# A transformer block's FFN on one core: SiLU as one ACT activation in half 1 and in the block products, and five plain weights split ahead instead of three

## The chip, the core and the metric

The kernel runs on one core of a Trainium2 chip. The core has five engines that the profile shows: PE (TensorE: matmuls, and PEld for their weight loads), DVE (VectorE), ACT (ScalarE), POOL (GpSimd) and SP, whose queue starts the DMA transfers here. Each engine works through its own queue in order; an instruction that waits holds up everything behind it in that queue. The metric is device time in microseconds (us), the median of several runs; lower is better.

## The reference, cut to what matters

The program computes one layer: sparse attention and an RWKV mixer, a gated merge, an output projection, and then the FFN, which alone the change touches:

```python
def _conv_ffn(h, w_up, conv_w, w_down):
    u = h @ w_up                       # 1024 x 1024 by 1024 x 5632
    u = conv(u, conv_w)                # causal, 3 taps, each channel by itself
    a, b = jnp.split(u, 2, axis=-1)    # 2816 channels each
    return (jax.nn.silu(a) * b) @ w_down
...
x = x + _conv_ffn(_rms_norm(x, norm_ffn[l]), ffn_up[l], ffn_conv[l], ffn_down[l])
```

SiLU is x times sigmoid(x), which is also 0.5 x (1 + tanh(x / 2)).

## The kernel before, in words

All products are made of float16 parts: an operand is split into hi (rounded) and lo (the rest), and each product is three matmuls, hi by hi, hi by lo and lo by hi. A weight tile of 128 x 1024 is loaded by SP into a raw buffer (`wraw`, two buffers in each of two pools), ACT writes its hi (`whi`, line 1602 in `split8`), and DVE its lo (`wlo`, line 1603). For the first two plain weights POOL makes the lo.

The FFN's 22 pairs of channel tiles (a tile of "a" channels with the matching tile of "b" channels) are worked in this way. The sequence of 1024 positions has two halves of 512.

- For pairs 0 to 5 (NE = 6) the halves are done apart, as plain products. Half 0 is filler work in earlier stages (`ffn0`, line 892 is its tanh). **Half 1** is the loop over `i in range(NE)`: per pair two plain weights (one of "a", one of "b"), each 24 matmuls; `taps` reads the result from PSUM into a tile u (ACT line 1529, two DVE taps line 1532, an edge line 1534); `silu` makes th = silu(ua) * ub with a tanh on ACT (1540) and two passes on DVE (1541, 1542), and SP stores th. u tiles have two buffers a kind. The weights come from `wslot`, which hands out pairs of hi and lo buffers in turn; PFD of them are split before the loop, and each step asks for one more. In the same loop DVE and ACT make the T tiles (`tprep`, lines 1557, 1558 and 1563): sums and differences of activations, split into hi and lo.
- For pairs 6 to 21 both halves go through **block products**: a scheme with seven half-size products instead of eight, each a group of 12 matmuls (`prod`, line 1669). The profile's PE rows carry the operands' names, so the groups of a product can be told apart. In PE's order they are: (1) weight "a" by h2h (`whi` by `h2h`); (2) `s12h` by T1; (3) the group `whi` by T4, which belongs to the "b" weight of the product before and is held back until here; (4) `s12h` by T2; (5) "a" by the second h2h; (6) `s34h` by T3; (7) `s34h` by `h2hi`.
- Between the groups ACT copies PSUM banks: line 1718 (bank b0 from a0, which group 4 adds to), 1721 (p5), 1725 (the **seed copy**, bank a1 from b0, after group 4 and before group 6 overwrites b0), 1733 (u3). DVE adds u3 and p5 in (1734, 1736), after which "a" of the product is complete and its taps start: U on ACT (1691), two taps on DVE (1693). `last`, a generator that is kept until the next product (`pend`), does the same for "b" and then makes TH = silu(U0) * U1 over all 1024 positions: tanh on ACT (1705), two passes on DVE (1706, 1707), two stores on SP (1709).
- The weights of the next products are prepared meanwhile by `prep_up`: it loads raw "a" and "b", POOL forms the sums s12 (1625, 1626) and s34 (1629, 1630), and `split8` splits "a", s12, s34 and the second half of "b" (a 128 x 512 `whi` and `wlo`). The buffers `whi`/`wlo` alternate between "a" and "b"; a raw buffer is free for a later load when its last reader has run.

Then the down projection follows, with its own weights and products (lines 1801 and 1872).

The order of the instructions in each engine's queue is made by a planner at build time: it takes the program's order as priority and places each instruction when it is ready by the planner's own model of durations. `tc.issue_after(x)` forces the instructions in its block to stand behind x in the queue of x's engine; it is an order, not a wait across engines. Inside the loop over the products the calls stand like this (shortened):

```python
prod(b0, w["12"], 4, TB[2], False)               # group 4
seed = A.activation(a1, b0, AF.Copy).ins         # 1725
if pend:
    next(pend)                                   # TH of the product before
wn = next(g_)                                    # raw loads, split of the next "a"
prod(a0, w["a"], 4, b21, False)                  # group 5
```

Of the kernel before, what the change touches and what calls it, by code (L numbers as in the profile page):

```python
# [11 lines left out]
AF = mybir.ActivationFunctionType  # L12
ALU = mybir.AluOpType
# [52 lines left out]
LV = 20  # L66
NEW = 4
TSTEPS = [(0, 0), (0, 1), (1, 1), (2, 2), (2, 3), (3, 3)]
PFD = 3
DSEQ = "nnsnsnsn"  # L70
GD = 6
GT = 7
# [96 lines left out]
def build(tc, D, dbg=None, upto=99):  # L169
    nc = tc.nc  # L170
    V, A, G, T = nc.vector, nc.scalar, nc.gpsimd, nc.tensor
# [5 lines left out]
    with ExitStack() as ctx:  # L177
        def pool(name, bufs=1, space=None, stack=ctx, **kw):
            if space is not None:
                kw["space"] = space  # L180
            return stack.enter_context(tc.tile_pool(name=name, bufs=bufs, reuse_waits="tile", **kw))
# [1343 lines left out]
        fp = pool("ffn", 1, stack=fst)  # L1525
# [11 lines left out]
        def silu(i, h, ua, ub):  # L1537
            th = fp.tile([128, 512], F32, name="th", tag="TH", bufs=2)
            with tc.issue_after(lasts[0]):
                t_ = A.activation(th, ua, AF.Tanh, scale=0.5)  # L1540
            V.scalar_tensor_tensor(th, th, 1.0, ua, op0=ALU.add, op1=ALU.mult)
            V.scalar_tensor_tensor(th, th, 0.5, ub, op0=ALU.mult, op1=ALU.mult)
            nc.sync.dma_start(th_d[h][i], th)
            return t_.ins

        lasts = [None]

# [35 lines left out]
        def wraw(src, scale="A", behind=None):  # L1583
            rn_[0] += 1
            x_ = rn_[0] // 2 % 2
            raw = (wp, fp)[x_].tile([128, 8, 128], F32, name="wraw", bufs=2)
            lastw[0] = load(raw, src).ins
            if scale == "A":
                with tc.issue_after(behind) if behind is not None else ExitStack():
                    A.activation(raw, raw, AF.Copy, scale=WS)  # L1590
            elif scale == "G":
                G.tensor_scalar(raw, raw, WS, 0.0, op0=ALU.mult, op1=ALU.add)
            return raw

        def split8(raw, ph, pl, th, tl, ks=slice(0, 8), e=None, **kw):
            hi = ph.tile([128, 8, 128], F16, name=th, **kw)
            lo = pl.tile([128, 8, 128], F16, name=tl, **kw)
            if e is G:
                lasts[0] = A.activation(hi[:, ks], raw[:, ks], AF.Copy).ins
                G.tensor_sub(lo[:, ks], raw[:, ks], hi[:, ks])  # L1600
            else:
                lasts[0] = A.activation(hi[:, ks], raw[:, ks], AF.Copy, scale=WS).ins  # L1602
                V.scalar_tensor_tensor(lo[:, ks], raw[:, ks], WS, hi[:, ks], op0=ALU.mult, op1=ALU.subtract)  # L1603
            return hi, lo

        wn_ = [0]

        def wslot(src):
            n = wn_[0] % 4
            wn_[0] += 1  # L1610
            e = V if WV[0] <= wn_[0] < WV[1] and wn_[0] % WV[2] == 0 else G
            raw = wraw(src, "G" if e is G else None)
            if n % 2 == 0:
                return split8(raw, wp, wp, "whi", "wlo", bufs=2, e=e)
            return split8(raw, fp, fp, ("s12h", "s34h")[n // 2], ("s12l", "s34l")[n // 2], e=e, bufs=2)

        lo4, hi4 = slice(0, 4), slice(4, 8)

        def prep_up(i):
            ra, rb = ((fp, wp)[i % 2].tile([128, 8, 128], F32, name="wraw", bufs=2) for _ in range(2))  # L1620
            load(ra, D["f_up"][i])
            lastw[0] = load(rb, D["f_up"][22 + i]).ins
            w = {"a": split8(ra, wp, wp, "whi", "wlo", bufs=2)}
            s12, s34 = (fp.tile([128, 8, 128], F32, name=n_) for n_ in ("s12", "s34"))
            G.tensor_add(s12[:, lo4], rb[:, lo4], rb[:, hi4])  # L1625
            G.tensor_sub(s12[:, hi4], s12[:, lo4], ra[:, lo4])  # L1626
            yield w
            w["12"] = split8(s12, fp, fp, "s12h", "s12l", bufs=2)
            G.tensor_sub(s34[:, lo4], ra[:, lo4], rb[:, lo4])  # L1629
            G.tensor_sub(s34[:, hi4], ra[:, hi4], s12[:, hi4])  # L1630
            yield
            w["34"] = split8(s34, fp, fp, "s34h", "s34l", bufs=2)
            yield
            w["b"] = split8(rb, wp, wp, "whi", "wlo", hi4, bufs=2)
            yield

        wq = [wslot(D["f_up"][22 * (n % 2) + n // 2]) for n in range(PFD)]
        for i in range(NE):
            us = []
            if i == NE - 1:  # L1640
                g_ = prep_up(NE)
                w = next(g_)
                next(g_)
            pjs = [ps("APMB"[(2 * i + o) % 4]) for o in range(2)]
            if i == 0 and LOL[3]:
                run(mm3s(list(zip(pjs, wq[:2])), h2hi[1], h2lo[1], 8, 1))
            for o in range(2):
                n = 2 * i + o + PFD
                if n < 2 * NE:
                    wq.append(wslot(D["f_up"][22 * (n % 2) + n // 2]))  # L1650
                hi, lo = wq.pop(0)
                u = utile(o, 1)
                pj = pjs[o]
                if i or not LOL[3]:
                    run(mm3(pj, hi, lo, h2hi[1], h2lo[1], 8))
                lasts[0] = taps(u, o, i, 1, pj)
                us.append(u)
            if i:
                silu(i - 1, 1, *prev)
            prev = us  # L1660
            with tc.issue_after(lasts[0]):
                for k in TSTEPS[i]:
                    next(tg[k])
        silu(NE - 1, 1, *prev)

        def prod(bank, w, o_, xs_, start):
            n = 0
            for k, wi, xi in [(k, 0, x_) for k in range(4) for x_ in (0, 1)] + [(k, 1, 0) for k in range(4)]:
                T.matmul(bank, w[wi][:, o_ + k], xs_[k][xi], start=start and n == 0, stop=n == 11,  # L1669
                         skip_group_check=True)  # L1670
                n += 1
# [13 lines left out]
        def wide(name):  # L1685
            return fp.tile([128, 1024], F32, name=name, tag=name, bufs=2)

        def taps2(o, i, c):
            ci = 22 * o + i
            u = wide(f"U{o}")  # L1690
            A.activation(u, c, AF.Copy, scale=P("conv", 88 + ci))  # L1691
            for d in (1, 2):
                V.scalar_tensor_tensor(u[:, d:1024], c[:, 0:1024 - d], P("conv", 44 * (2 - d) + ci), u[:, d:1024],  # L1693
                                       op0=ALU.mult, op1=ALU.add)
            return u
# [3 lines left out]
        def last(i, w, ua, cc):  # L1699
            b0 = cc[:, 0:512]  # L1700
            prod(b0, w["b"], 4, TB[4], False)
            ub = taps2(1, i, cc)
            yield
            th = wide("TH")
            lt_[0] = A.activation(th, ua, AF.Tanh, scale=0.5).ins
            V.scalar_tensor_tensor(th, th, 1.0, ua, op0=ALU.add, op1=ALU.mult)
            V.scalar_tensor_tensor(th, th, 0.5, ub, op0=ALU.mult, op1=ALU.mult)
            for h in range(2):
                nc.sync.dma_start(th_d[h][i], th[:, H[h]])
            yield  # L1710

        pend, lt_ = None, [None]
        for i in range(NE, 22):
            g_ = prep_up(i + 1) if i < 21 else iter([None] * 4)
            ca, cb_ = (pall[:, b_:b_ + 1024] for b_ in (1024 * (i % 2), 2048 + 1024 * (i % 2)))
            a0, a1, b0, b1 = ca[:, 0:512], ca[:, 512:1024], cb_[:, 0:512], cb_[:, 512:1024]
            prod(a0, w["a"], 0, b11, True)
            A.activation(b0, a0, AF.Copy)
            prod(b1, w["12"], 0, TB[1], True)
            p5 = fp.tile([128, 512], F32, name="p5")  # L1720
            A.activation(p5, b1, AF.Copy)
            if pend:
                next(pend)
            prod(b0, w["12"], 4, TB[2], False)
            seed = A.activation(a1, b0, AF.Copy).ins
            if pend:
                next(pend)
            wn = next(g_)
            prod(a0, w["a"], 4, b21, False)
            next(g_)  # L1730
            prod(b0, w["34"], 0, TB[3], False)
            u3 = fp.tile([128, 512], F32, name="u3")
            A.activation(u3, b0, AF.Copy)
            V.tensor_add(b1, b1, u3)
            prod(a1, w["34"], 4, b22, False)
            V.tensor_add(a1, a1, p5)
            pend = last(i, w, taps2(0, i, ca), cb_)
            next(g_)
            next(g_)
            w = wn  # L1740
        run(pend)
        t_ = lt_[0]
# [245 lines left out]
```

## Time and profile before

| | |
|---|---|
| median of 3 runs (lowest to highest) | 1710.64 us (1709.13 to 1712.36) |
| the profiled execution, its whole time | 1718.26 us |
| its span, first to last instruction | 1716.3 us |
| mean granted clock of PE, whole span | 0.986 |
| PE / DVE / ACT / POOL busy | 1646.6 / 1196.7 / 917.1 / 431.6 us |
| half 1's products | from about 1125 to 1187 us |
| block products | from 1188.6 to about 1494 us |

Times in rows are counted from the span's start. In a timeline a row gives start, length, engine, line, operation, output and inputs; square brackets give the idle time just before and what ended it. "issue" there means that the engine waited for nothing that the profile shows. A row of a group gives busy time and mean ns of one after the bar. Matmuls are pipelined: the length of one (0.38 us) runs over the start of the next.

### The profile page before, as it was taken

How to read it: one execution, taken by the hardware profiler on the slowest of the kernel's cores; microseconds unless marked ns; L12 is line 12 of the kernel's file. 1: busy time of each engine (PE TensorE's matmuls, PEld its weight loads, DVE VectorE, ACT ScalarE, POOL GpSimd, SP SyncE). 2: the span in 40 equal slices, each digit the busy share in tenths (PEclk: the TensorE clock that was granted, in tenths of full speed). 3: DMA queues.
4: the chain of work that ended last, by engine and by line, in shares of the span. 5: the costliest groups of instructions: out<-in, count | busy, mean ns of one | idle time of the engine just before them, and what ended most of it. 6: DMA issues, size and time to landing. Idle time of an engine off the chain costs nothing.

```text
span 1716.3 us, 30297 instructions
## 1 busy us (share of the span) xinstructions
PE 1646.6 (96%) x11856; PEld 864.1 (50%) x11856; DVE 1196.7 (70%) x1978; ACT 917.1 (53%) x1625; POOL 431.6 (25%) x352
## 2 busy tenths in 40 slices
PE   8999999999999999998989999999999999999997
PEld 3446555555555545665655534444444444444443
DVE  6545577778876657954446585499867777786898
ACT  6664675757667645455446464454444544645530
POOL 2101131121112110000004200123333333456756
PEclk9999999999999999998999999999999999999999
DMA  6242343242444474435345673543222222534402
GB/s 221 91 136 90 96 145 115 78 135 60 130 141 134 129 235 156 137 118 173 124 143 184 205 280 104 175 151 129 86 86 74 81 92 87 213 113 129 135 25 99
DMA packets 124687, 224.62 MB, mean 131 GB/s; under 512 B 16384, under 2 KB 45440, under 8 KB 124416
## 3 DMA queue, kind: packets, MB, share of 16 engines
q1 hardware_dynamic: 124544, 222.69, 39.4%
q8 instruction: 93, 1.52, 0.4%
q14 instruction: 50, 0.41, 0.1%
HBM read 153.86 MB, written 63.96 MB: 127 GB/s over the span
## 4 chain that ended last, share of the span: by engine, by line
PE 40%; DVE 11%; DMA 7%; ACT 5%; issue 4%; POOL 4%; DVEq 0%; POOLq 0%; SPq 0%; ACTq 0%
PE pall L271 15%; PE pall L1801 5%; PE pall L1669 5%; PE pall L1872 4%; PE pall L291 2%; DMA wraw<-f_up 2%; DMA zs<-sg_d 2%; POOL s L1629 1%; PE pall L1220 1%; POOL s L1625 1%; DVE s12l L1603 1%; PE pall L1164 1%; POOL s L1626 1%; PE pall L1311 1%; DVE wlo L1603 1%
## 5 line engine op out<-in xcount | busy, mean ns | idle before, releaser
L271 PEld LDWEIGHTS <-whi 128*128 128x128 f16 x1840 | 177.3, 98 | 211.5 <-issue 14.7
L271 PE MATMUL pall<-hlo,whi 128*128 128x512 f16 x608 | 229.6, 379 | 2.1 <-DVE hlo L246 2.1
L271 PE MATMUL pall<-hhi,whi 128*128 128x512 f16 x608 | 229.1, 379 | 2.0 <-ACT ad L981 1.5
L261 DVE SCALAR_TENSOR_TENSOR wlo<-wraw,whi 128x1024 f16<-128x1024 f32 (+1 forms) x98 | 111.0, 1133 | 65.3 <-ACT whi L259 35.9
L271 PE MATMUL pall<-hhi,wlo 128*128 128x512 f16 x608 | 154.5, 382 | 0.0
L665 DVE TENSOR_TENSOR pl<-pf,ph 128x512 f16<-128x512 f32 (+3 forms) x208 | 117.3, 573 | 36.9 <-ACT pf L664 36.2
L259 ACT ACTIVATE whi<-wraw 128x1024 f16<-128x1024 f32 (+1 forms) x98 | 92.7, 948 | 91.7 <-PE pall L271 66.8
L271 PEld LDWEIGHTS <-wlo 128*128 128x128 f16 x920 | 88.0, 98 | 100.1 <-issue 4.6
L663 ACT ACTIVATE ph<-pall 128x512 f16<-128x512 f32 (+3 forms) x208 | 99.6, 479 | 64.6 <-PE pall L658 32.7
L600 DVE TENSOR_REDUCE mp<-pall 128x1 f32<-128x512 f32 (+2 forms) x192 | 95.8, 515 | 35.6 <-PE pall L598 26.3
L664 ACT ACTIVATE pf<-pall 128x512 f32<-128x512 f32 (+3 forms) x208 | 100.0, 481 | 0.0
L1693 DVE SCALAR_TENSOR_TENSOR U<-pall,par,U 128x1023 f32<-128x1023 f32 x64 | 82.0, 1282 | 8.1 <-ACT U L1691 6.2
L1625 POOL TENSOR_TENSOR s<-wraw 128x512 f32<-128x512 f32 x16 | 25.7, 1608 | 220.5 <-DMA wraw<-f_up 207.5
L1602 ACT ACTIVATE s12h<-s 128x1024 f16<-128x1024 f32 x16 | 16.9, 1057 | 95.9 <-POOL s L1626 94.9
L1393 POOL TENSOR_TENSOR b<-b,bonus 128x512 f32<-128x512 f32 x8 | 10.7, 1343 | 224.7 <-ACT b L1391 196.7
L668 PEld LDWEIGHTS <-ph 128*128 128x128 f16 x592 | 56.1, 97 | 16.0 <-ACT ph L663 2.8
L673 PEld LDWEIGHTS <-pl 128*128 128x128 f16 x592 | 55.9, 99 | 15.8 <-DVE pl L665 7.1
L687 POOL TENSOR_TENSOR onat<-onat,ot 128x256 f32<-128x256 f32 x32 | 27.6, 868 | 138.9 <-DVE ot L686 109.3
L1669 PEld LDWEIGHTS <-whi 128*128 128x128 f16 x384 | 37.5, 98 | 46.7 <-ACT u L1529 1.7
L671 PEld LDWEIGHTS <-ph 128*128 128x128 f16 x592 | 56.2, 98 | 6.0 <-issue 1.7
L1803 DVE SCALAR_TENSOR_TENSOR acc<-pall,acc 128x512 f32<-128x512 f32 x80 | 51.8, 678 | 8.6 <-PE pall L1801 8.5
L1603 DVE SCALAR_TENSOR_TENSOR wlo<-wraw,whi 128x1024 f16<-128x1024 f32 (+1 forms) x37 | 50.4, 1362 | 1.9 <-PE pall L1669 1.2
(596 smaller groups left out, 4469.7 us busy)
## 6 DMA issues: line engine op xcount, KB each, us to landing
wraw<-f_up SPq DMA_DIRECT2D x56, 512.0 KB, 3.4
wraw<-w_t SPq DMA_DIRECT2D x46, 512.0 KB, 3.8
wraw<-f_dn SPq DMA_DIRECT2D x22, 512.0 KB, 3.8
sg_d<-zs SPq DMA_DIRECT2D x32, 256.0 KB, 2.2
wraw<-w_out SPq DMA_DIRECT2D x16, 512.0 KB, 3.6
th_d<-TH SPq DMA_DIRECT2D x32, 256.0 KB, 2.3
z_d<-zs SPq DMA_DIRECT2D x28, 256.0 KB, 2.9
x<-xT SPq DMA_DIRECT2D x24, 256.0 KB, 5.6
```

What stands on the lines that cost most here:

```text
L259: A.activation(hi[:, :nk], raw, AF.Copy, scale=WS)
L261: V.scalar_tensor_tensor(lo[:, :nk], raw, WS, hi[:, :nk], op0=ALU.mult, op1=ALU.subtract)
L271: lastm[0] = T.matmul(ps, a[:, k], ks_(b, k), start=(n == 0), stop=(n == 3 * nk - 1)).ins
L600: V.reduce_max(mp[:, x, br, t:t + 1], pm[:, 0:(b1 - b0) * 128], axis=AX.X)
L663: A.activation(ph[0:nkey, rg], pa[0:nkey, rg], AF.Exp, scale=0.125)
L664: A.activation(pf[0:nkey, rg], pa[0:nkey, rg], AF.Exp, scale=0.125)
L665: V.tensor_sub(pl[0:nkey, rg], pf[0:nkey, rg], ph[0:nkey, rg])
L1603: V.scalar_tensor_tensor(lo[:, ks], raw[:, ks], WS, hi[:, ks], op0=ALU.mult, op1=ALU.subtract)
L1669: T.matmul(bank, w[wi][:, o_ + k], xs_[k][xi], start=start and n == 0, stop=n == 11, skip_group_check=True)
L1693: V.scalar_tensor_tensor(u[:, d:1024], c[:, 0:1024 - d], P("conv", 44 * (2 - d) + ci), u[:, d:1024], op0=ALU.mult, op1=ALU.add)
L1801: T.matmul(pj, x[:, m], y, start=(n == 0), stop=(n == 5))
L1872: T.matmul(pj, w[x][:, 4 * kp + j], hs[kp][y], start=(n == 0), stop=(n == 5))
```

## The change

Three edits. In half 1 and in the block products the tanh and the two DVE passes become one SiLU activation on ACT and one plain product on DVE. In the block products that SiLU is made to stand behind the seed copy of the product in which it runs (`lt_[1]`); before, the tanh had no such place. And PFD goes from 3 to 5, with `wslot` handing out buffers in a round of three (whi, s12, s34, two buffers each) where it was a round of four (whi, s12, whi, s34). Half 0 (`ffn0`) keeps its tanh.

```diff
-PFD = 3
+PFD = 5
...
         def silu(i, h, ua, ub):
             th = fp.tile([128, 512], F32, name="th", tag="TH", bufs=2)
             with tc.issue_after(lasts[0]):
-                t_ = A.activation(th, ua, AF.Tanh, scale=0.5)
-            V.scalar_tensor_tensor(th, th, 1.0, ua, op0=ALU.add, op1=ALU.mult)
-            V.scalar_tensor_tensor(th, th, 0.5, ub, op0=ALU.mult, op1=ALU.mult)
+                A.activation(th, ua, AF.Silu)
+            V.tensor_mul(th, th, ub)
             nc.sync.dma_start(th_d[h][i], th)
-            return t_.ins
...
         def wslot(src):
-            n = wn_[0] % 4
+            n = wn_[0] % 3
             wn_[0] += 1
             e = V if WV[0] <= wn_[0] < WV[1] and wn_[0] % WV[2] == 0 else G
             raw = wraw(src, "G" if e is G else None)
-            if n % 2 == 0:
+            if n == 0:
                 return split8(raw, wp, wp, "whi", "wlo", bufs=2, e=e)
-            return split8(raw, fp, fp, ("s12h", "s34h")[n // 2], ("s12l", "s34l")[n // 2], e=e, bufs=2)
+            return split8(raw, fp, fp, ("s12h", "s34h")[n - 1], ("s12l", "s34l")[n - 1], e=e, bufs=2)
...
             th = wide("TH")
-            lt_[0] = A.activation(th, ua, AF.Tanh, scale=0.5).ins
-            V.scalar_tensor_tensor(th, th, 1.0, ua, op0=ALU.add, op1=ALU.mult)
-            V.scalar_tensor_tensor(th, th, 0.5, ub, op0=ALU.mult, op1=ALU.mult)
+            with tc.issue_after(lt_[1]):
+                lt_[0] = A.activation(th, ua, AF.Silu).ins
+            V.tensor_mul(th, th, ub)
             for h in range(2):
                 nc.sync.dma_start(th_d[h][i], th[:, H[h]])
             yield
...
-        pend, lt_ = None, [None]
+        pend, lt_ = None, [None, None]
...
-            seed = A.activation(a1, b0, AF.Copy).ins
+            seed = lt_[1] = A.activation(a1, b0, AF.Copy).ins
```

## The prediction

> **What bounds the kernel now.** I read the page's head first, then the busy time by stretch, the waits of PE, PE's and ACT's timelines over one block product, and the chain of waits there.
>
> ```profile
> span 1716.3 us, 30297 instructions
> PE 1646.6 (96%) x11856; PEld 864.1 (50%) x11856; DVE 1196.7 (70%) x1978; ACT 917.1 (53%) x1625; POOL 431.6 (25%) x352
> ```
>
> PE bounds the whole: about 70 us of the span are without a matmul, and only what lies in the FFN can be won here. The stretches (span; then PE, PEld, DVE, ACT, POOL busy; clock; DMA share; GB/s):
>
> ```profile
> 1185.00:1205.00 20.00, 14.17 (x65) 6.01 (x64) 20.00 (x26) 10.33 (x15) 10.23 (x7) 1.00 0.45 159
> 1205.00:1285.00 80.00, 80.00 (x372) 36.29 (x371) 59.51 (x52) 35.63 (x46) 25.12 (x16) 1.00 0.26 89
> 1285.00:1470.00 185.00, 179.34 (x817) 79.74 (x816) 137.92 (x119) 86.31 (x111) 58.62 (x37) 1.00 0.25 86
> 1470.00:1700.00 230.00, 227.90 (x1050) 102.55 (x1049) 184.35 (x236) 107.75 (x164) 149.30 (x107) 1.00 0.32 109
> ```
>
> The clock is full, so lost time is waiting. PE stands at two places: at the passage from half 1 into the block products (5.8 us of 20) and in the later block products (5.7 of 185). What PE waited for between 1130 and 1520 us, longest first (line, releaser: total, times, longest):
>
> ```profile
> PE pall L1669 <- ACT pall L1725: 4.4, 10, 0.4
> PE pall L1669 <- ACT pall L1718: 1.9, 1, 1.9
> PE pall L1669 <- DVE T2l L1558: 1.9, 1, 1.9
> ```
>
> The ten waits for L1725, the seed copy, are one per block product, and they understate the loss. PE's first matmuls of a product, of its second group, and of the next product:
>
> ```profile
> 1338.79 0.38 PE L1669 MATMUL pall<-h2h,whi 128*128 128x512 f16 x1
> ...
> 1341.38 0.38 PE L1669 MATMUL pall<-T1h,s12h 128*128 128x512 f16 x1
> ...
> 1357.82 0.38 PE L1669 MATMUL pall<-h2h,whi 128*128 128x512 f16 x1
> ```
>
> A group of 12 matmuls takes 2.59 us, so seven groups need 18.13; the product takes 19.03. Each of ten products loses 0.9, together **8.9 us**. At the passage the four standstills, with the 0.16 by which a matmul's modelled end runs on (0.38 against 2.59/12 = 0.22), come to 5.8 + 4 x 0.16 = **6.5 us**. So 15.4 us is all this change can win by waiting less.
>
> Why 19.03? The chain of waits over the same time shows a ring (start, length):
>
> ```profile
> 1332.24 0.70 DVE wlo L1603
> 1332.93 0.02 issue
> 1332.95 3.16 DMA wraw<-f_up
> ...
> 1336.28 1.82 POOL s L1625
> 1338.09 2.21 POOL s L1629
> 1340.30 1.24 POOL s L1626
> ...
> 1341.56 1.07 ACT s12h L1602
> ...
> 1342.65 1.31 DVE s12l L1603
> 1343.96 0.61 DVE pall L1734
> 1344.57 0.61 DVE pall L1736
> ```
>
> wlo of the 512-wide "b" weight is the last reader of a raw buffer. Its end starts the load of a later weight, POOL sums that, ACT and DVE split the sum, and only behind that split, in DVE's order, come the additions L1734 and L1736 that finish the running product. ACT goes on:
>
> ```profile
> 1326.18 1.11 ACT L1691 ACTIVATE U<-pall,par 128x1024 f32<-128x1024 f32 x1 [1.16 <-DVE pall L1736]
> 1327.19 0.59 ACT L1718 ACTIVATE pall<-pall 128x512 f32<-128x512 f32 x1
> 1330.01 1.06 ACT L1705 ACTIVATE TH<-U 128x1024 f32<-128x1024 f32 x1 [2.23 <-issue]
> 1330.97 0.58 ACT L1721 ACTIVATE p<-pall 128x512 f32<-128x512 f32 x1
> 1331.45 0.62 ACT L1602 ACTIVATE whi<-wraw 128x512 f16<-128x512 f32 x1
> 1331.97 1.11 ACT L1691 ACTIVATE U<-pall,par 128x1024 f32<-128x1024 f32 x1
> 1332.97 0.60 ACT L1725 ACTIVATE pall<-pall 128x512 f32<-128x512 f32 x1
> ```
>
> The tanh (L1705) waits 2.23 us for DVE's two taps, and p, whi of "b", the U of "b" and the seed stand behind it on ACT. DVE puts its first tanh product ahead of wlo too. That closes the ring at 19.02 (wlo 1332.24, next 1351.26): it, and not PE, sets the pace.
>
> **The change, part by part.**
>
> (1) *The block products' SiLU behind the seed.* ACT loses nothing in count (one activation for one), but p, whi of "b", U and seed no longer wait for the taps. Count from a product's first matmul. The fourth group starts at 3 x 2.59 = 7.77; the third, which reads the old wlo of "b", ends there, so wlo cannot be written sooner. It now can be written just then, at 7.8: whi stands ahead of U on ACT and p is long free, and DVE is through its taps, which take
>
> ```profile
> 1327.33 2.60 DVE L1693 SCALAR_TENSOR_TENSOR U<-pall,par,U 128x1023 f32<-128x1023 f32 x2
> ```
>
> from 1.15 after U's start. Before, wlo began at 1351.26 - 1338.79 = 12.5, so it comes 4.7 us earlier. From wlo's start to the next U is 1345.20 - 1332.24 = 13.0 (U stands one period of 19.02 behind 1326.18), and from there to the end of L1718 1327.78 - 1326.18 = 1.6. So L1718 ends at 7.8 + 14.6 = 22.4, that is 4.2 into the next product; PE wants it at 7.77. **The ring has 3.5 us to spare, and PE paces itself at 18.13.**
>
> What is late next? The seed, after the fourth group (10.4), ends at 11.0 and PE wants it at 12.95. The SiLU runs 11.0 to 12.0, whi of the next "a" behind it to 13.1, and wlo of "a", behind DVE's TH product (12.1 to 13.3), by 16.1 (2.8 us, an estimate: the 0.70 of the half-wide wlo, doubled for the width and again for a slow neighbour); PE wants that at 18.13 + 8 x 0.22 = 19.9. The two stores of TH follow the product on SP; the load that waits for "a"'s wlo stands behind them and has a whole product to land. The SiLU itself is no operation of the trace: nearest is the tanh of the same shape (1.06), which I take; at twice that, the spare 3.8 us still cover it. Gain 8.9, if the queues come out like this; bounds 0 and 8.9.
>
> (2) *One product for two on DVE.* Per block product one pass goes. It had 1.3 us apiece:
>
> ```profile
> L1707 DVE SCALAR_TENSOR_TENSOR TH<-TH,U 128x1024 f32<-128x1024 f32 x16 | 21.1, 1320 | 0.5
> ```
>
> DVE is free for 47 of 185 us there, so beyond the ring this is worth nothing. In half 1 it counts, for there DVE is full:
>
> ```profile
> 1112.00:1208.00 96.00, 90.17 (x417) 40.48 (x416) 95.62 (x131) 50.10 (x77) 30.04 (x16) 1.00 0.42 142
> ```
>
> 95.6 of 96 us, and the standstills at the passage are waits for what DVE brings late (T1l and T2l directly, the bank copies through u tiles that its products hold). Five SiLUs lie before the last of them:
>
> ```profile
> L1542 DVE SCALAR_TENSOR_TENSOR th<-th,u 128x512 f32<-128x512 f32 x5 | 5.5, 1110 | 0.0
> L1541 DVE SCALAR_TENSOR_TENSOR th<-th,u 128x512 f32<-128x512 f32 x5 | 3.9, 779 | 0.0
> ```
>
> A plain product for the pair frees between 3.9 and 5.5, less the 0.07 that neighbours overlap: 3.5 to 5.1. I take 3.6, the low end: L1542 has the shape of L1541 and is longer by 0.33, which I put down to POOL working beside it, and that will slow another pass instead.
>
> (3) *Five weights ahead.* No instruction is added or removed. The twelve plain weights go round whi, s12, s34 with two buffers each; whi alone, every second turn, had held it to four. The later weights are split up to two products (2 x 24 x 0.216 = 10.4 us) sooner, their raw buffers come free sooner, and with them the loads, POOL sums and splits of the first block product, on which ACT stood blocked with u copies behind it. But DVE is full, so what moves forward pushes taps and T tiles back: I count it at 0, between -3 (the order hurts T2l) and +2.9 (all 6.5 gone, with (2)).
>
> (4) *The table.* One load at the first SiLU, near 1148:
>
> ```profile
> L1501 ACT ACT_TABLE_LOAD x1 | 1.3, 1283 | 0.0
> ```
>
> ACT is half idle there (50 of 96), so 0; uncovered, 1.3. The ACT rows above show tanh among copies without a load between. The Trainium skill ("ScalarE: Activation LUTs", Table sets: the hidden batching unit) tells to batch activations by set, since each switch costs a load, and that cheap functions such as copy are in every set. By the first half, read alone, the change would be a loss; by the second, one switch suffices. Its price (same page, What ACT_TABLE_LOAD costs) is 2.66 us with the drain; by that the sum would move by nothing or, uncovered, 2.7.
>
> **Sum:** 8.9 + 3.6 + 0 + 0 = 12.5 us. From 1470 PE is busy 227.9 of 230 us, so the gain reaches the end whole. The profiled execution took 1718.26 (span 1716.3), 7.6 above the median of the runs, 1710.64, so it would come to 1705.8, and the median to **1698**.
>
> **Rivals.**
>
> *A: only the loop gains.* The passage stays DVE's, its 3.6 eaten by the new order or worse, down to -3: gain 5.9 to 8.9, 1702 to 1705. For: DVE is full. Against: work really goes away. Taps of "b" ahead of its wlo land here too: wlo starts at 8.9 + 2.6 = 11.5, the ring needs 18.3, a loss of about 0.2 a product. So does a table that lacks copy: two loads of 1.3 per SiLU put the split of "a" at 18.7, still before 19.9, and hurt half 1 alone; if they take half of the 6 x 2.6 us from where ACT is late, the passage's 3.6 and 4 more are gone, 1706.
>
> *B: the ring stays.* Another in-order neighbour takes the tanh's place, and the product still takes 18.9; only the passage gains: 1707. For: DVE's and ACT's order is the planner's and is planned anew. Against: every member is ready earlier.
>
> *C: slower.* On DVE the TH product lands ahead of wlo of "b" (or its stores ahead of that weight's load on SP). Then wlo hangs on the seed: from the fourth group, 2.59 + 0.6 + 1.1 + 1.2 + 14.6, with some 0.2 of hand-over, is 20.3 against 18.13. That bites from about the third product on: 13 x 2.1 = 27 lost for 8.9 before, less 3.6: +15, 1725. It decides once wlo starts over 3.5 us after the third group. For: the tanh product stands ahead of wlo today. Against: it stands there because it was ready first; now wlo is ready at 7.8, the product at 12.0.
>
> **How the numbers follow.** Forecast 0.70, A 0.10, B 0.09, C 0.11. What can be told from no change is 0.2%, 3.4 us. Forecast and A are faster (0.80), B the same (0.09; it lies at the edge), C slower (0.11). The forecast's own range is 1694 (all 15.4 and a little) to 1702; with A and B it ends at 1710. C stays out.
>
> **What would show it.** Right: PE's starts of successive products 18.1 apart to the end; no wait for L1725; wlo of "b" within 1 us of the third group's end; no standstill over 1 us at the passage; DVE some 0.6 us less per half-1 SiLU; one more table load. Wrong: a product still near 19, or DVE holding wlo for the TH product.

## The result, and the profile after

| | before | after |
|---|---|---|
| first comparison, median (lowest to highest) | 1711.14 us (1709.13 to 1712.36), 4 runs | 1701.01 us (1699.11 to 1703.55), 4 runs |
| ratio, 95% interval | | 0.9943 (0.9926 to 0.996) |
| second comparison, median (lowest to highest) | 1711.87 us (1708.77 to 1716.88), 11 runs | 1698.15 us (1694.59 to 1700.95), 6 runs |
| ratio, 95% interval | | 0.9916 (0.990 to 0.9933) |
| profiled execution of the first: whole time, span | 1718.26, 1716.3 us | 1703.55, 1701.8 us |

The change makes the kernel faster, by 10.1 us in the first comparison and 13.7 in the second. The forecast was 1698, 12.5 less than before.

The head of the page of the changed kernel:

```profile
span 1701.8 us, 30292 instructions
...
PE 1640.8 (96%) x11856; PEld 863.7 (51%) x11856; DVE 1174.4 (69%) x1956; ACT 923.3 (54%) x1626; POOL 435.6 (26%) x352
```

DVE works 22.3 us less in 22 instructions fewer (one pass for two, 6 + 16 times), ACT has one instruction more, a table load. The same stretches as before, each moved to where the work now lies (span; then PE, PEld, DVE, ACT, POOL busy; clock; DMA share; GB/s):

```profile
1183.00:1203.00 20.00, 17.66 (x82) 7.81 (x81) 18.35 (x26) 8.45 (x13) 7.05 (x5) 1.00 0.51 172
1203.00:1283.00 80.00, 80.00 (x372) 36.28 (x371) 57.94 (x49) 39.94 (x49) 27.93 (x16) 1.00 0.24 86
1283.00:1468.00 185.00, 185.00 (x859) 83.87 (x857) 133.47 (x111) 93.86 (x114) 64.45 (x37) 1.00 0.27 95
1468.00:1690.00 222.00, 219.74 (x1011) 98.63 (x1009) 176.92 (x231) 100.34 (x154) 149.85 (x109) 1.00 0.31 109
```

In the stretch of 185 us PE now has no idle time at all, where 5.7 us were lost. At the passage it is idle for 2.3 us of 20, where it was 5.8. What PE waited for between 1130 and 1520 us:

```profile
PE pall L1667 <- DVE T1l L1556: 1.9, 1, 1.9
PE pall L1667 <- ACT pall L1716: 0.5, 1, 0.5
```

The ten waits for the seed copy are gone. PE's first matmul of the second group in three products one behind another:

```profile
1297.36 0.38 PE L1667 MATMUL pall<-T1h,s12h 128*128 128x512 f16 x1
...
1315.49 0.38 PE L1667 MATMUL pall<-T1h,s12h 128*128 128x512 f16 x1
...
1333.62 0.38 PE L1667 MATMUL pall<-T1h,s12h 128*128 128x512 f16 x1
```

18.13 and 18.13: seven groups of 2.59 without a gap, and so to the last product.

For the comparisons below I add up PE's standstills from the start of half 1 to the end of the block products: the time from one matmul's start to the next, less the usual 0.22. Before, that is 6.49 us at the passage and 8.81 in the loop, 15.30 together; after, it is 2.65 and 0. **12.65 us went.** The span fell by 14.5, because half 1 also began 1.35 us sooner (its first matmul at 1122.04 for 1123.39), which is well within what this start moves between two executions of one kernel (last section). From the second group of the last product to the end it is 241.7 us before and 241.2 after, so nothing is given back later.

### The profile page after: what moved, and what is told of

Same layout as the page of the kernel before. It is cut to its first block, busy times and chain, and to the rows that moved or that the text cites. A ratio compares the mean times of both kernels' runs of the same rounds, so it can differ in the third digit from the quotient of the medians.

```text
span 1701.8 us, 30292 instructions
## 1 busy us (share of the span) xinstructions
PE 1640.8 (96%) x11856; PEld 863.7 (51%) x11856; DVE 1174.4 (69%) x1956; ACT 923.3 (54%) x1626; POOL 435.6 (26%) x352
## 5 line engine op out<-in xcount | busy, mean ns | idle before, releaser
L271 PEld LDWEIGHTS <-whi 128*128 128x128 f16 x1808 | 173.6, 98 | 205.6 <-issue 11.4
L1667 PEld LDWEIGHTS <-whi 128*128 128x128 f16 x384 | 37.6, 98 | 45.3 <-issue 0.2
```

Source lines behind the costliest of these rows:

```text
L271: lastm[0] = T.matmul(ps, a[:, k], ks_(b, k), start=(n == 0), stop=(n == 3 * nk - 1)).ins
```

## The experiments

"Passage" and "loop" are the two sums of standstills just defined; a standstill repeats closely (2.65 and 2.66 at the passage in two profiled executions of the changed kernel), while the whole time of one execution moves by several us for another reason (last section). So where a kernel was run only once, its verdict rests on the standstills. They are sums of waits alone; what the table leaves out in e1, e5 and e9 stands behind it.

| kernel | half 1 | block products | plain weights ahead | passage | loop | products apart |
|---|---|---|---|---|---|---|
| before | tanh, 2 passes | tanh, no place | 3 | 6.49 | 8.81 | 19.02 later |
| after | SiLU | SiLU behind seed | 5 | 2.65 | 0 | 18.13 |
| e1 | tanh, 2 passes | tanh behind seed | 3 | 6.54 | 0 | 18.13 |
| e2 | SiLU | SiLU, no place | 5 | 2.65 | 8.74 | 19.02 later |
| e8 | SiLU | SiLU ahead of p | 5 | 2.68 | 8.58 | 19.02 later |
| e10 | tanh, 2 passes | tanh (behind p), sums' splits later | 3 | 3.56 | 0 | 18.13 |
| e3 | SiLU | SiLU behind seed, wlo of "b" behind TH | 5 | 2.67 | 0.45 | 18.13 |
| e9 | SiLU | tanh, no place | 3 | 3.97 | 8.45 | 19.02 later |
| e5 | tanh, 2 passes | SiLU behind seed | 5 | 4.06 | 0 | 18.13 |
| e4 | SiLU | SiLU behind seed | 3 | 2.19 | 0 | 18.13 |
| e7 | SiLU | SiLU behind seed, T tiles first | 5 | 1.49 | 0 | 18.13 |
| e11 | SiLU | SiLU behind seed, T tiles first | 3 | 2.04 | 0 | 18.13 |

In the single executions of e1, e5 and e9 the granted clock also stood at one half for 3.4 us, right behind a standstill at the passage (from 1206.9, 1193.0 and 1197.7 us). In e1 (behind the busy times: clock, DMA share, GB/s):

```profile
1207.00:1210.00 3.00, 3.00 (x9) 1.07 (x8) 0.29 (x1) 0.00 (x0) 0.00 (x0) 0.50 0.00 0
```

Matmuls began 0.43 us apart there instead of 0.22, which cost another 1.6 us in each of the three. With it the passage lost 8.2 us in e1, 5.7 in e5 and 5.6 in e9. Before the change and in e10, with standstills of 2.1 us at the same place, the clock stayed at 1.00. Each of the three was run once, so whether these 1.6 us belong to their edits is open, and the comparisons at the passage below are given with and without them.

**The order alone.** The old kernel, with its tanh and two passes, and only the place behind the seed added:

```diff
-            lt_[0] = A.activation(th, ua, AF.Tanh, scale=0.5).ins
+            with tc.issue_after(lt_[1]):
+                lt_[0] = A.activation(th, ua, AF.Tanh, scale=0.5).ins
...
-            seed = A.activation(a1, b0, AF.Copy).ins
+            seed = lt_[1] = A.activation(a1, b0, AF.Copy).ins
```

> The kernel before with one edit: in the block products the tanh is put behind the seed copy; tanh and both DVE passes stay, half 1 and the weights too. Theory (the place of the activation closes or opens the ring): products 18.1 us apart, no waits for the seed copy, about 8.9 us less; the passage keeps its 6.5 us. Rival (it is DVE's saved pass that frees the ring): products stay at 19.0.

The stretch of 185 us in the loop, and what PE waited for from half 1 to the end of the products:

```profile
1285.00:1470.00 185.00, 185.00 (x859) 83.86 (x858) 156.11 (x123) 93.74 (x115) 73.05 (x37) 1.00 0.27 94
```

```profile
PE pall L1669 <- ACT pall L1726: 2.8, 1, 2.8
PE pall L1669 <- ACT pall L1719: 1.9, 1, 1.9
PE pall L1669 <- ACT u L1529: 1.2, 1, 1.2
```

The whole loss of the loop is gone with both DVE passes still there (DVE is busy for 156 of 185 us, more than before). The three waits left are single ones, all at the passage, and come to what the passage lost before. One execution took 1708.83 us, beside 1710.9 for the kernel before; that is less than the 8.8 us of standstill that went. Of the difference 1.6 us are the half clock at the passage; more cannot be read from one execution each.

**The order taken away.** The changed kernel without the place for its SiLU, and, as a second run, with the SiLU put expressly where the tanh of before stood, ahead of p and whi of "b":

```diff
-            with tc.issue_after(lt_[1]):
-                lt_[0] = A.activation(th, ua, AF.Silu).ins
+            lt_[0] = A.activation(th, ua, AF.Silu).ins
```

> The changed kernel without the order behind the seed copy: the planner places the block products' SiLU by itself; in the order it made, the SiLU stands behind whi of 'b' and ahead of U of 'b' and of the seed. Theory: wlo of 'b' no longer hangs on the SiLU, so the ring (about 16.7 us by its members) stays under PE's 18.13 and products are 18.1 apart, as in the changed kernel. Rival (the stated order itself is what gains): back to 18.9 to 19.0, about 8 us more than the changed kernel.

```diff
+            th = wide("TH")
+            lt_[0] = A.activation(th, ua, AF.Silu).ins
+            yield
             prod(b0, w["b"], 4, TB[4], False)
             ub = taps2(1, i, cc)
             yield
-            th = wide("TH")
-            with tc.issue_after(lt_[1]):
-                lt_[0] = A.activation(th, ua, AF.Silu).ins
...
-            A.activation(p5, b1, AF.Copy)
+            if pend:
+                next(pend)
+            with tc.issue_after(lt_[0]) if pend else ExitStack():
+                A.activation(p5, b1, AF.Copy)
```

> The changed kernel with the SiLU at the tanh's old place on ACT: ahead of p, whi of 'b', U of 'b' and seed. One DVE pass as in the changed kernel. Theory: the ring is U to taps 3.8, SiLU 1.1, p 0.5, whi 0.6, wlo to the next U 13.0, together 18.9, over PE's 18.13, so products drift to 18.9 apart once the slack of 3.5 us is used up (some five products), and 6 to 8 us are lost against the changed kernel. Rival (the saved DVE pass is what matters): 18.1 apart, no loss.

Both go back to 19.02, and lose 8.74 and 8.58 us in the loop. For the first of them I had misjudged the order: behind whi of "b" is where the SiLU stood in the first product, the only one I had looked at, while in the later ones the planner put it where the tanh had been. ACT in a later product of that kernel (left to the planner):

```profile
1336.93 0.59 ACT L1715 ACTIVATE pall<-pall 128x512 f32<-128x512 f32 x1
1339.75 1.06 ACT L1703 ACTIVATE TH<-U 128x1024 f32<-128x1024 f32 x1 [2.23 <-issue]
1340.71 0.58 ACT L1718 ACTIVATE p<-pall 128x512 f32<-128x512 f32 x1
1341.19 0.62 ACT L1600 ACTIVATE whi<-wraw 128x512 f16<-128x512 f32 x1
```

Again 2.23 us of waiting for the taps, with p and whi behind it. And the chain of waits of the second kernel (SiLU expressly ahead of p), over one turn of the ring:

```profile
1340.14 0.53 ACT whi L1600
...
1340.69 0.70 DVE wlo L1601
...
1341.41 3.13 DMA wraw<-f_up
...
1344.71 1.98 POOL s L1623
1346.68 2.21 POOL s L1627
1348.89 1.23 POOL s L1624
...
1359.71 0.70 DVE wlo L1601
```

From wlo to wlo 19.02, as in the kernel before, although DVE has no tanh product ahead of wlo any more. So the pass that the change saves in the loop buys nothing there while the ring is closed: the ring closes over ACT, and the order is the whole gain of the loop. One execution each took 1708.78 and 1706.94 us, beside 1710.9 before.

**The ring shortened at another place.** The old kernel, with its tanh still ahead of whi of "b", its U and the seed; the splits of s12 and s34 are ordered behind the additions of the running product, so that these additions no longer wait for the loaded weight:

```diff
-            next(g_)
+            with tc.issue_after(fin[0]) if fin else ExitStack(), tc.issue_after(fin[1]) if fin else ExitStack():
+                next(g_)
...
-            A.activation(u3, b0, AF.Copy)
+            uc = A.activation(u3, b0, AF.Copy).ins
...
-            V.tensor_add(a1, a1, p5)
+            fin = uc, V.tensor_add(a1, a1, p5).ins
```

> The kernel before with another link of the ring cut: tanh and two passes stay at the old place, but the split of s12 is put behind the additions (u3 copy on ACT, the second addition on DVE) of the product before. In the order made, both sums' splits stand between the additions and U's taps. Theory: additions and U (2.3 us) leave the ring, the split of s34 (1.2) enters: 19.0 - 2.3 + 1.2 = 17.9, just under PE's 18.13, so products are 18.1 to 18.3 apart and 7 to 9 us are gained in the loop; the passage keeps about 6.5. Rival (the tanh's place delays PE through the seed copy alone, with no ring): products stay at 19.0.

```profile
1285.00:1470.00 185.00, 185.00 (x858) 83.83 (x857) 134.91 (x120) 97.59 (x119) 64.58 (x39) 1.00 0.27 97
```

In this stretch PE has no gap, and the products stand 18.13 apart to the end. DVE in one product:

```profile
1328.62 0.70 DVE L1737 TENSOR_TENSOR pall<-pall,p 128x512 f32<-128x512 f32 x1 [1.26 <-PE pall L1669]
1329.23 1.22 DVE L1603 SCALAR_TENSOR_TENSOR s12l<-s,s12h 128x1024 f16<-128x1024 f32 x1
```

The addition now waits for PE, and the split comes behind it. The ring is not open, for on ACT the next U (1330.17) still stands behind the splits s12h and s34h (1327.86 and 1329.21); but it closes in less than PE's 18.13, since whi of "b" waits for PE in it, by 0.19 us (1335.53). Shortened at another member, the same ring frees the loop as the change does. That is the strongest support for the ring as the cause: no SiLU is in this kernel, and its tanh still holds up whi of "b". The planner did put the tanh behind p. By itself that would take the 0.5 us of p (1330.97 to 1331.45 before) out of 19.02 and leave about 18.5, an estimate, still above 18.13. The kernel has a gain at the passage too, 3.56 for 6.49, which I had not looked for. One execution took 1701.41 us, beside 1710.9.

**wlo of "b" held behind the TH product**, the order of rival C:

```diff
-            V.tensor_mul(th, th, ub)
+            lt_[2] = V.tensor_mul(th, th, ub).ins
...
+            if late:
+                with tc.issue_after(lt_[2]):
+                    next(late)
...
-            next(g_)
+            late = g_
```

> The changed kernel with wlo of 'b' forced behind the TH product on DVE, the order of rival C. The planner answers by placing the split of s12 behind the additions and U's taps, so that additions and U no longer wait for POOL. Theory (only the ring counts, and this order opens it at the split): products 18.13 apart, no loss. Rival C as priced (a late wlo costs whatever the rest of the order): 20.2 apart, some 25 us more than the changed kernel.

DVE over one product of it:

```profile
1300.96 1.23 DVE L1705 TENSOR_TENSOR TH<-TH,U 128x1024 f32<-128x1024 f32 x1 [0.41 <-ACT TH L1704]
1302.10 1.82 DVE L1601 SCALAR_TENSOR_TENSOR wlo<-wraw,whi 128x512 f16<-128x512 f32 x2
1305.19 0.70 DVE L1735 TENSOR_TENSOR pall<-pall,u 128x512 f32<-128x512 f32 x1 [1.27 <-ACT u L1734]
...
1309.04 2.60 DVE L1691 SCALAR_TENSOR_TENSOR U<-pall,par,U 128x1023 f32<-128x1023 f32 x2 [1.18 <-ACT U L1689]
1312.30 1.31 DVE L1601 SCALAR_TENSOR_TENSOR s12l<-s,s12h 128x1024 f16<-128x1024 f32 x1 [0.66 <-ACT s12h L1600]
```

wlo does stand behind the TH product, and the products still come 18.13 apart. But the planner, given the later weight, also put s12l behind the additions and the taps: the order of the experiment before. The 0.45 us lost in its loop is one gap, before a matmul of the down projection. So this run does not test the price of C (1725 us), which supposed the rest of the order unchanged; it shows that one late member costs nothing once the additions are out of the ring. A late wlo with the additions still behind s12l was not tried. One execution took 1698.18 us, beside 1713.46.

**The passage, edit by edit.** The SiLU of half 1 alone on the old kernel; then the changed kernel with the old half 1 (and five weights ahead); then the changed kernel with three weights ahead:

```diff
-                t_ = A.activation(th, ua, AF.Tanh, scale=0.5)
-            V.scalar_tensor_tensor(th, th, 1.0, ua, op0=ALU.add, op1=ALU.mult)
-            V.scalar_tensor_tensor(th, th, 0.5, ub, op0=ALU.mult, op1=ALU.mult)
+                A.activation(th, ua, AF.Silu)
+            V.tensor_mul(th, th, ub)
```

(The second run takes these lines back from the changed kernel.) And the third, against the changed kernel:

```diff
-PFD = 5
+PFD = 3
...
-            n = wn_[0] % 3
+            n = wn_[0] % 4
...
```

> The kernel before with the SiLU and one pass in half 1 alone; three weights ahead, block products as before. Theory: the ring is untouched, late products 19.02 apart; the passage stands 2.5 to 3.5 us instead of 6.5, and from half 1's first matmul to the last block product 3 to 4 us are saved, as the ring starts sooner too. Rival (the ring takes the passage's gain back, since its first U comes no sooner): under 1 us saved over that stretch.

> The changed kernel with half 1's tanh and two DVE passes back; five weights ahead and the block products' SiLU stay. Products 18.13 apart. Theory (saved passes carry the passage): standstills there 5.5 to 7 us. Rival (five weights ahead carry it): about 3 us.

> The changed kernel with three weights split ahead and the round of four, as before; both SiLUs and the place behind the seed stay. Products 18.13 apart. Theory (the passage gains by DVE's saved passes, the weights ahead are worth about 0): standstills at the passage 2.5 to 3.5 us, against 6.5 before and 2.7 in the changed kernel. Rival (the weights ahead relieve the passage): 5 to 6.5 us.

Half 1's SiLU alone takes the passage from 6.49 to 3.97 us and leaves the loop at 19.02; with the other edits there already (e5 to the changed kernel) it takes 4.06 to 2.65. So by waits it is worth 2.5 alone and 1.4 on top of the others; with the half clock of e9 and e5 counted in, it is 0.9 alone (6.5 to 5.6) and 3.1 on top (5.7 to 2.65).

e9 missed what was expected of it. Its passage stands longer than the 2.5 to 3.5 us of the theory, and from half 1's first matmul to the second group of the last product it saves 1.3 us (351.2 before, 349.9 in e9) where the theory said 3 to 4 and the rival under 1. In e5 the passage lies between theory (5.5 to 7) and rival (about 3) by waits, and inside the theory's range with the half clock. Against e1 it is 2.5 us less by either count. Between e1 and e5 lie both the five weights and the SiLU of the block products, and the two runs do not part them.

With half 1's SiLU there, e9, e4 and the changed kernel do. The block products' SiLU behind the seed takes the passage from 3.97 (5.6 with the half clock) to 2.19, a little under the 2.5 expected of e4, and five weights ahead instead of three take it to 2.65, so they gain nothing there. What an edit is worth at the passage thus depends on which others are there; whether the edits cover the same loss is not shown, since the sizes move by 1.6 us with the half clock. One execution each took 1713.7, 1704.4 and 1701.46 us, beside 1713.46.

**The rest of the passage.** Of the 2.65 us that remain, 2.01 are PE's wait for T1l. DVE at that place in the changed kernel:

```profile
1188.20 1.22 DVE L1601 SCALAR_TENSOR_TENSOR s12l<-s,s12h 128x1024 f16<-128x1024 f32 x1
...
1190.86 1.22 DVE L1601 SCALAR_TENSOR_TENSOR s34l<-s,s34h 128x1024 f16<-128x1024 f32 x1
...
1193.67 1.75 DVE L1556 TENSOR_TENSOR T3l<-t,T3h 128x512 f16<-128x512 f32 x1
...
1196.48 0.68 DVE L1556 TENSOR_TENSOR T1l<-t,T1h 128x512 f16<-128x512 f32 x1
```

Two splits for the next product stand ahead of T tiles that PE wants at once. So I ordered the first splits of the loop behind the last T tile, once with five and once with three weights ahead, and ran the changed kernel again beside them in five rounds:

```diff
+        tlast = [None]
...
-                V.tensor_sub(lo, t, hi)
+                tlast[0] = V.tensor_sub(lo, t, hi).ins
...
-            wn = next(g_)
+            with tc.issue_after(tlast[0]) if i == NE else ExitStack():
+                wn = next(g_)
```

(The two calls of `next(g_)` that follow in that product have the same line.)

> The changed kernel with the splits of product 7's sums (s12, s34, 2 x 1.2 us of DVE) put behind the last T tile of the passage. Theory (the passage's rest is DVE doing what is wanted later): the wait of 2.0 us for T1l goes to under 0.5, standstills at the passage from 2.7 to about 0.7, products still 18.13 apart, 2 us less than the changed kernel. Rival (the late splits then hold up the second product): the same 2 us lost there.

> The same order with three weights ahead and the round of four. Theory (the weights ahead are worth nothing once half 1 has the SiLU): standstills at the passage 0.3 to 1.2 us, time within 1 us of the run with five ahead. Rival: 1.5 us or more slower.

> The changed kernel once more, beside the kernel before in five rounds. Theory: standstills of PE in the FFN fell from 15.3 us to 2.7 us, so 12.6 us less, ratio about 0.9926. If the smaller difference of the medians seen first (10.1 us) is real, about 2.5 us were given back elsewhere, and the ratio stays near 0.994.

With five weights the wait for T1l falls to 1.32 (under 0.5 was expected) and the passage to 1.49, about twice what I had expected to remain; with three the passage is 2.04, above the 0.3 to 1.2 expected. In time: 1697.61 us (1697.09 to 1700.84; ratio to before 0.9918, 0.9902 to 0.9935) and 1700.86 (1698.86 to 1701.27; 0.993, 0.9916 to 0.9945), beside 1698.15 for the changed kernel. By the medians the kernel with three ahead is 3.25 us slower than the one with five, which is the mark that its rival named (1.5 us or more). Their standstills differ by 0.55 us only and their intervals overlap, so what the five weights are worth behind this order is open. The 1.2 us that e7 saves by its standstills cannot be told from nothing, so there is no version here that measurably beats the changed kernel.

## Why the prediction was right, step by step

**The size.** Forecast 12.5 us; standstills 12.65 less; medians 10.1 and 13.7 less. By the intervals of the ratios these two are 6.8 to 12.7 and 11.5 to 17.1, and 12.65 lies in both, in the first just so. That the forecast comes within 0.2 us of the standstills is in part luck, as (2) and (3) show.

**(1) The loop: predicted 8.9, measured 8.81.** ACT and DVE over one product of the changed kernel, which begins at 1294.77:

```profile
1298.11 1.11 ACT L1689 ACTIVATE U<-pall,par 128x1024 f32<-128x1024 f32 x1 [1.16 <-DVE pall L1734]
1299.12 0.59 ACT L1716 ACTIVATE pall<-pall 128x512 f32<-128x512 f32 x1
...
1301.88 0.63 ACT L1600 ACTIVATE whi<-wraw 128x512 f16<-128x512 f32 x1 [1.13 <-PE pall L1667]
...
1305.33 0.58 ACT L1723 ACTIVATE pall<-pall 128x512 f32<-128x512 f32 x1 [1.48 <-PE pall L1667]
1305.83 1.05 ACT L1704 ACTIVATE TH<-U 128x1024 f32<-128x1024 f32 x1
1307.06 1.06 ACT L1600 ACTIVATE whi<-wraw 128x1024 f16<-128x1024 f32 x1 [0.18 <-PE pall L1667]
```

```profile
1302.81 0.69 DVE L1601 SCALAR_TENSOR_TENSOR wlo<-wraw,whi 128x512 f16<-128x512 f32 x1 [0.95 <-PE pall L1667]
1303.89 2.60 DVE L1691 SCALAR_TENSOR_TENSOR U<-pall,par,U 128x1023 f32<-128x1023 f32 x2 [0.39 <-ACT U L1689]
1306.91 1.22 DVE L1705 TENSOR_TENSOR TH<-TH,U 128x1024 f32<-128x1024 f32 x1 [0.41 <-ACT TH L1704]
1308.15 2.19 DVE L1601 SCALAR_TENSOR_TENSOR wlo<-wraw,whi 128x1024 f16<-128x1024 f32 x1
```

Counted from the product's first matmul: wlo of "b" starts at 8.04 (predicted 7.8, and it waits for PE alone, as it should), the seed ends at 11.14 (11.0), the SiLU runs from 11.06 to 12.11 (11.0 to 12.0), whi of "a" ends at 13.35 (13.1) and its wlo at 15.57 (16.1). The copy into b0 (L1716) ends 4.94 into the product, not 4.2: what lies between wlo and the next U takes 13.55 here, not 13.0. PE wants it at 7.77, so 2.8 us are to spare and not 3.5. The mechanism that was foreseen is the one that acts: PE paces itself, and the experiments put the gain of the loop on the order alone.

**(2) One product for two: predicted 3.6 at the passage, nothing in the loop.** In the loop that held (e1, e2, e8). The passage gained 3.84 in all, so the sum came out, but not by this term alone: half 1's SiLU by itself measured 2.5 by waits and 0.9 with the half clock (e9). The block products' SiLU, counted at nothing at the passage, added 1.8 by waits (e9 to e4). The step that was mis-sized is the one that turned freed DVE time into earlier T tiles one for one: the passes of half 1's six SiLUs take DVE 10.8 us before and 5.3 in e9, so 5.5 us were freed and at most 2.5 of them reached PE. Part of what is freed goes to splits that the planner puts ahead of the T tiles; with these put behind them (e7) the passage falls by another 1.2.

**(3) Five weights ahead: counted at 0, with bounds of -3 and +2.9.** With the other edits it measures -0.5 (2.19 to 2.65), and +0.55 with the T tiles first (2.04 to 1.49), so 0 was near enough. Where half 1 keeps its tanh it is not known: e5 has 2.5 us less than e1 for it and the block products' SiLU together.

**(4) The table: one more load, hidden.** ACT at half 1's first SiLU:

```profile
1145.39 1.28 ACT L1540 ACT_TABLE_LOAD   x1
1146.69 0.63 ACT L1540 ACTIVATE th<-u 128x512 f32<-128x512 f32 x1
1147.22 0.61 ACT L1555 ACTIVATE T2h<-t 128x512 f16<-128x512 f32 x1
```

The one load stays the only one for all 22 SiLUs, with copies between them, and PE has no standstill there: its only two lie at the passage, behind 1183. This agrees, for the one set that SiLU uses here, with the sentence of the Trainium skill ("ScalarE: Activation LUTs", Table sets: the hidden batching unit) that copy is in every set.

**The rivals.** B did not happen in the changed kernel, and e2 shows how near it was: without its stated place the SiLU goes back to the tanh's, and the product to 19.02. A's order, taps of "b" ahead of its wlo, did not come: wlo starts 1.1 us before the taps. C did not come either; its price is untested.

**The marks to look for.** Products 18.13 apart, no wait for the seed, wlo within 1 us of the third group's end, one more load: all seen. DVE works 0.9 us less per half-1 SiLU (10.8 to 5.2 us for six), more than the 0.6 named. "No standstill over 1 us at the passage" was wrong: 2.01 us before T1l remain, behind two splits and a slowed T3l.

## What to carry to other kernels

When a loop runs slower than its bounding engine and the wait named is short and the same each time, follow the chain of waits until it comes back to its own instruction: the period is then the sum of a ring through queues that work in order, and the price is the difference of the two periods, not the wait. Such a ring stops setting the pace when one waiting instruction moves behind work that is ready; a pass saved beside the ring buys nothing until then, and where the program leaves the place to a planner, state it. What an edit is worth can depend on which others are there, so try each alone and each left out, and look at the granted clock as well as at the waits before comparing single executions.

## What the runs showed that was not expected

**DVE and POOL take turns.** The old passes were 1320 ns each on average; the one product that took their place is longer:

```profile
L1705 DVE TENSOR_TENSOR TH<-TH,U 128x1024 f32<-128x1024 f32 x16 | 28.0, 1749 | 6.2 <-ACT TH L1704 6.2
```

POOL beside the DVE rows of step (1):

```profile
1307.11 2.15 POOL L1623 TENSOR_TENSOR s<-wraw 128x512 f32<-128x512 f32 x1 [11.32 <-DMA wraw<-f_up]
1309.22 2.24 POOL L1627 TENSOR_TENSOR s<-wraw 128x512 f32<-128x512 f32 x1
1311.42 1.26 POOL L1624 TENSOR_TENSOR s<-s,wraw 128x512 f32<-128x512 f32 x1
```

POOL's first sum ends 1.13 us after DVE's product does (1309.26 and 1308.13); DVE's wlo ends 1.12 after POOL's second sum begins (1310.34 and 1309.22); that sum ends 1.12 after wlo does (1311.46 and 1310.34). With nothing beside it POOL's next sum takes 1.26, and a DVE split of this size took 1.22 above. Each thus looks as if it waited for the other's whole instruction and then ran at its usual speed, not as if both ran slowly. The Trainium skill ("SBUF — State Buffer", SBUF: two separate sides) states just this: a DVE operation with two SBUF inputs and a POOL operation that reads SBUF hold a shared port in turn, for a whole instruction. These rows agree; no experiment here took POOL's sums away.

**The start of half 1 moves by 10 us between two executions of one kernel.** Its first matmul came at 1122.04 in the first profile of the changed kernel and at 1112.32 in the second; before it was 1123.39, and in the other kernels between 1116 and 1121.5. The stretch from 750 to 1000 us, first before, then after, then after again:

```profile
750.00:1000.00 250.00, 230.81 (x2473) 140.63 (x2472) 127.49 (x238) 128.37 (x227) 40.83 (x28) 0.93 0.53 173
```

```profile
750.00:1000.00 250.00, 230.92 (x2478) 141.08 (x2476) 128.75 (x240) 129.29 (x228) 39.42 (x28) 0.94 0.53 175
```

```profile
750.00:1000.00 250.00, 230.87 (x2481) 140.39 (x2478) 136.21 (x253) 130.40 (x233) 40.38 (x28) 0.97 0.54 181
```

The granted clock of PE differs between executions of the same work, and the sooner start goes with the higher clock. Of the 9.7 us between the two executions of the changed kernel 3.8 were there at 750 us already. Up to 1112 us the clock stood at one half for 37.5 us in the first and for 20.5 in the second; since matmuls begin twice as far apart then (0.43 and 0.22 us in e1), the 17 us between them cost 8.5, an estimate. That is most of the 9.7. Whether it is the whole cause is open, and the record does not say that both ran on one chip. The 9.7 us are as large as the effect that was measured, which is why one execution of each kernel cannot rank them, and their standstills within the changed stretch can, where the clock was full.
